# Padding the small block products of a DeltaNet inverse to 128 rows, with another load order at the start and another split of the last scaling

## The chip, the core and the metric

The kernel runs on one core of one Trainium2 chip. Its metric is the device time of one execution in microseconds (us). The engines are TensorE (PE, matrix products, with its weight loads shown apart as PEld), VectorE (DVE), ScalarE (ACT), GpSimd (POOL) and SyncE (SP), which here issues nearly all DMAs. Matrix products read SBUF and write PSUM. "L358" in the profile is the line of a helper through which nearly all instructions are recorded, so groups are told apart by the names of their tiles: `pz<-wc,dt` writes tile pz and reads wc and dt.

## What is computed

The reference is a decoder block on x of 1024 tokens by 1024 features, in float32:

```python
h = rmsnorm(x, norm1_w)
proj = h @ w_in                       # sb_q, sb_k, sb_v, sb_z, g_q, g_k, g_v, g_z, g_b, g_a
o_sb  = rmsnorm(stick_breaking_attention(sb_q, sb_k, sb_v)) * silu(sb_z)   # 8 heads of 64
o_gdn = rmsnorm(gated_delta_chunked(...)) * silu(g_z)                      # 4 heads of 128
y = x + concat(o_sb, o_gdn) @ w_out
return rmsnorm(y, final_norm_w)
```

The gated delta rule works on chunks of tokens. In each chunk a unit lower triangular system `(I + A) s = r` is solved, where A holds the decayed products of the keys with each other. The kernel uses chunks of 128 tokens, eight for each head, and forms the inverse X of the triangular matrix explicitly.

## The kernel before, in words

Large products keep float32 accuracy by splitting each operand in a high part (float32r) and a low part (the rest) and adding three products: high by high, high by low, low by high (`mm3`, lines 586 to 589). Names that end in h and l are such parts.

**The start (lines 631 to 664).** The transposed x comes in eight bands k of 128 rows (tile `xr`, 512 KB), and so does the part of the input weight that makes the attention's queries (tile `w`, named wq in the profile, 256 KB). For each band ACT makes the high parts `xh` and `wh` (wqh), DVE the low parts `xl` and `wl` (wql); x is scaled by the norm's gain on the way. Eight PSUM accumulators `qp[j]`, j = 2 i + half, hold the product for 128 columns i of the weight and one half of the 1024 tokens. Band 0 is loaded in halves, in the order: tokens 0 to 511 of x, columns 0 to 255 of the weight, tokens 512 to 1023, columns 256 to 511. Its 24 products are issued pair by pair, (0, 2), (1, 3), (4, 6), (5, 7): the second pair needs the second half of x, the third the second half of the weight. The second half's low part of x is tied behind the low part of its weight by `later` (line 654). From band 1 on each band is loaded in two DMAs and all eight accumulators take three products each.

At line 735 three DMAs clear scratch in DRAM that the inverse uses: `xd0` gets a small identity, and each `xds` gets 128 KB of zeros. They are recorded with priority 0.

**The planner.** Python simulates the engines while the program is built (classes `Model`, `Recorder`, `Pool`, lines 58 to 372, and `interleave`, line 440). Every instruction is recorded with a cost and a priority (smaller is earlier); DVE, ACT, POOL and SP each take, of the instructions that are ready in the simulation, the one with the smallest priority, and this order is written into the program for good. PE's instructions run in the order in which they are recorded. `interleave` chooses between streams (generators) whenever PE's list is empty: a stream may continue when what it waits for should have ended. Streams with priority 100 and above (the projections, and later the output's products) fill PE when no other is ready. The planner adds 150 ns where a product has another number of weight rows, in classes of 32, 64 and 128, than the one before (line 331). Once built, the order on each engine is fixed and the engines wait for each other by semaphores. A DMA of SP that comes eight DMAs later uses the same semaphore again, and waits for the older one to land.

**The inverse (`gdn_inv`, lines 1099 to 1176), once for each of four heads.** `nm` (a view of tile dt, 128x128 for each of the eight chunks) holds minus A, transposed. The inverses of the diagonal blocks of 32x32 are made by POOL and DVE and exchanged through DRAM; line 1125 loads them as `xc`, and DVE transposes each to `wc`. The blocks of 64x64 follow by products of 32x32 blocks, and from these the whole of 128x128:

- First group (lines 1137 to 1142): for both diagonal blocks of 64 rows and each of eight chunks, nm's off-diagonal block of 32x32 by wc. In the profile `pz<-wc,dt`. DVE copies the result to `y1` (tile name y).
- Second group (lines 1153 to 1160): 16 products of y1 by xc and 8 of xc by y1, which give the off-diagonal blocks and, for one of them, its transpose: `pz<-xc,y` and `pz<-y,xc`.
- Then 8 products with nm's columns 64 to 127 over all 128 rows (`pz<-wy,dt`), for which `wy` is padded with zeros, and 8 by X (`pz<-xinv,wy`).

Each of these float32 products shows as two weight loads and two matmuls, which the text calls passes.

**The end (`products_attention`, lines 1500 to 1550).** For the last block of 128 tokens the output row is cut in parts of 512, 320 and 192 columns. After each product DVE adds x, and the squares are summed (ACT for the first two, DVE for the last). POOL multiplies by the final gain (DVE for the last part), adds the sums and EPS, and takes the power -0.5 (`rsqrt`). Then line 1535 has DVE scale columns 0 to 543, line 1536 ACT columns 640 to 1023, line 1537 POOL columns 544 to 639; SP stores columns 0 to 639 and ACT's queue the rest.

Of the kernel before, what the change touches and what calls it, by code (L numbers as in the profile page):

```python
# [25 lines left out]
EPS = 1e-6  # L26
# [447 lines left out]
def block(tc, xT_d, x_d, n1_d, wE_d, wQ_d, wC_d, conv_d, alog_d, dtb_d, mixw_d, wo_d, fnw_d, out_d):  # L474
# [4 lines left out]
    with ExitStack() as top:  # L479
# [155 lines left out]
        raw, loads = [], {}  # L635
        for k in range(NK):
            w = s0.tile([P, 512], F32, tag="wcr", bufs=6, name="wq")
            wh = s0.tile([P, 512], F32R, tag="wqh", bufs=2, name="wqh")
            wl = s0.tile([P, 512], F32R, tag="wql", bufs=2, name="wql")
            xr = fx.tile([P, T], F32, f"xr{k}", "kq") if k < 4 else s0.tile([P, T], F32, name=f"xr{k}")  # L640
            raw.append(xr)
            n = 1 if k else 2
            for u in range(n):
                hs, es = slice(u * 512, T // n + u * 512), slice(u * 256, 512 // n + u * 256)
                loads.setdefault(f"k{k}", []).extend([S.dma_start(xr[:, hs], xT_d[k * P:(k + 1) * P, hs]), S.dma_start(w[:, es], wQ_d[:, k, es])])
                if k == 0 and u == 0:
                    V.tensor_copy(wh[:, es], w[:, es])
                else:
                    A.activation(wh[:, es], w[:, es], AF.Copy)
                low = V.tensor_tensor(wl[:, es], w[:, es], wh[:, es].bitcast(F32), ALU.subtract)  # L650
                A.activation(xh[:, k, hs], xr[:, hs], AF.Copy, scale=n1[:, k:k + 1])
                xlow = V.scalar_tensor_tensor(xl[:, k, hs], xr[:, hs], n1[:, k:k + 1], xh[:, k, hs].bitcast(F32), ALU.mult, ALU.subtract)
                if k == 0:
                    later(xlow, low)
            if k:
                for j in range(8):
                    i, hs = j // 2, slice((j % 2) * 512, (j % 2) * 512 + 512)
                    es = slice(i * P, (i + 1) * P)
                    mm3(qp[j], wh[:, es], wl[:, es], xh[:, k, hs], xl[:, k, hs], False, k == NK - 1)
                continue  # L660
            for pair in ((0, 2), (1, 3), (4, 6), (5, 7)):
                for a, (lw, rx) in enumerate(((wh, xh), (wl, xh), (wh, xl))):
                    for j in pair:
                        TE.matmul(qp[j], lw[:, (j // 2) * P:(j // 2) * P + P], rx[:, 0, (j % 2) * 512:(j % 2) * 512 + 512], start=a == 0, stop=False)
# [67 lines left out]
        V.memset(ones, 1.0)  # L732
        G.affine_select(triu, ones, pattern=[[1, P]], compare_op=ALU.is_ge, fill=0.0, base=0, channel_multiplier=-1)

        S.dma_start(xd0, ident[0:16, 0:16])
        V.memset(zero, 0.0)
        for t in xds:
            S.dma_start(t[0:32768].rearrange("(p u f) -> p u f", p=P, u=2), zero.unsqueeze(1).to_broadcast([P, 2, P]))
        s0_ctx.close()


# [357 lines left out]
        def gdn_inv(h):  # L1099
# [21 lines left out]
            times(yx, xa, nb)  # L1121
            times(xa[:, :, 16:32], yx, xb)
            S.dma_start(rows, xa.rearrange("p r i -> p (r i)"))
            xc = gd.tile([P, 8, 32], F32, tag="xc", name="xc")
            yield S.dma_start(xc, xd[0:32768].rearrange("(g c b r i) -> (b r) (g c) i", g=2, c=4, b=4, r=32, i=32))
            wc = gd.tile([P, 8, 32], F32, tag="wc", name="wc")
            r = V.transpose(wc.rearrange("p c i -> p (c i)"), xc.rearrange("p c i -> p (c i)"))
            wy = gd.tile([P, 8, 64], F32, tag="br", name="wy")
            W = wy[0:64]
            G.memset(W[0:32, :, 32:64], 0.0)  # L1130
            G.memset(wy[64:128], 0.0)
            V.tensor_copy(W[0:32, :, 0:32], wc[0:32])
# [2 lines left out]

            quads = [slice(32 * q, 32 * q + 32) for q in range(4)]
            y1p = pz()
            yv = y1p[:, 0:256].rearrange("p (c i) -> p c i", c=8)
            for q in range(2):
                o = 64 * q  # L1140
                for c in range(8):
                    TE.matmul(yv[o + 32:o + 64, c, :], nm(c, slice(o, o + 32), slice(o + 32, o + 64)), wc[o:o + 32, c, :], start=True, stop=True)
            y1 = gd.tile([P, 8, 32], F32, tag="yt", name="y1")
            for q in range(2):
                o = 64 * q
                r = V.tensor_copy(y1[o + 32:o + 64], yv[o + 32:o + 64])
            yield lambda: h == 0 or f"c{2 * h - 1}" in flags
            for q in range(4):
                A.activation(X[quads[q], :, quads[q]], xc[quads[q]], AF.Copy)
# [5 lines left out]
            for q in range(2):  # L1155
                o = 64 * q
                for c in range(8):
                    TE.matmul(xv[o:o + 32, c, :], y1[o + 32:o + 64, c, :], xc[o + 32:o + 64, c, :], start=True, stop=True)
            for c in range(8):
                TE.matmul(xv[32:64, c, :], xc[32:64, c, :], y1[32:64, c, :], start=True, stop=True)  # L1160
            r = V.tensor_copy(W[32:64, :, 0:32], xv[32:64])
            for q in range(2):
                o = 64 * q
# [336 lines left out]
        def products_attention():  # L1500
            yield lambda: f"d{NB - 1}" in flags
            for b in range(NB):
                last = b == NB - 1
                parts = (slice(0, 512), slice(512, 832), slice(832, D)) if last else (slice(0, 512), slice(512, D))
                sy = None
                for got in product(b, 0, parts):
                    if not isinstance(got, tuple):
                        yield got
                        continue
                    n, hs, yp, y = got  # L1510
                    if sy is None:
# [8 lines left out]
                    if last:  # L1520
                        (V if n == 2 else G).tensor_tensor(yf[:, hs], y[:, hs], wts["fnw"][:, hs], ALU.mult)
                    if n and last:
                        G.tensor_tensor(sy[:, 0:1], sy[:, 0:1], sy[:, n:n + 1], ALU.add)
                        if n == 1:
                            G.tensor_scalar(sy[:, 0:1], sy[:, 0:1], EPS, None, ALU.add)
                    elif n:
                        V.scalar_tensor_tensor(sy[:, 0:1], sy[:, 0:1], EPS, sy[:, n:n + 1], ALU.add, ALU.add)
                    if n < len(parts) - 1:
                        yield
                        continue  # L1530
                    ry = pools[0].tile([P, 1], F32, tag="ry", bufs=2, name="ry")
                    os_ = slice(b * P, (b + 1) * P)
                    if last:
                        rsqrt(ry, sy[:, 0:1], 1)
                        V.tensor_scalar(yf[:, 0:544], yf[:, 0:544], ry[:, 0:1], None, ALU.mult)
                        A.activation(yf[:, 640:D], yf[:, 640:D], AF.Copy, scale=ry[:, 0:1])
                        G.tensor_scalar(yf[:, 544:640], yf[:, 544:640], ry[:, 0:1], None, ALU.mult)
                        S.dma_start(out_d[os_, 0:640], yf[:, 0:640])
                        nc.scalar.dma_start(out_d[os_, 640:D], yf[:, 640:D])
# [57 lines left out]
```

## Time and profile before

| | us |
|---|---|
| median of 3 runs (650.01 to 651.02) | 650.99 |
| the profiled execution's own time | 651.54 |
| its span, first to last instruction | 649.6 |
| PE busy in it | 639.3 |
| DVE, ACT, POOL busy | 422.4, 393.7, 341.8 |
| PE's first product, last product's start | 1.67, 643.24 |

All rows of the profile come from that one execution, whose time is 0.55 us above the median. In a listing by time the columns are the start from the beginning of the span, the duration, the engine, the line, the operation, the tiles written and read, weights' rows*columns for PE, the shape, the number of instructions merged in the row, and in brackets the idle time ahead of it with what ended it. SPq and ACTq are the engines' issues of DMAs. PE overlaps consecutive matmuls, so what one costs is read from the distance between starts rather than from its duration.

### The profile page before, as it was taken

The page shows a single profiled execution, that of the slowest core. Times are in us where ns is not written, and L with a number is a line of the kernel's source. Part 1 is how long each engine was busy: PE and PEld are TensorE (multiplying, and loading weights), DVE is VectorE, ACT ScalarE, POOL GpSimd, SP SyncE. Part 2 cuts the span into 40 slices and gives each one's busy share as a digit, 9 for nine tenths or more (in the row PEclk, how much of TensorE's full clock was granted, in tenths as well). Part 3 has the DMA queues.
Part 4 walks back from the last instruction along what each step waited for, and adds up shares of the span by engine and source line. Part 5 has one row for each costly group of instructions (what it writes and reads, how often), then busy time and mean ns, then how long its engine had stood idle before and what let it go on. Part 6 is the DMA issues. An engine that isn't in the chain of part 4 may idle for free.

```text
span 649.6 us, 11680 instructions
## 1 busy us (share of the span) xinstructions
PE 639.3 (98%) x3976; PEld 549.7 (85%) x3976; DVE 422.4 (65%) x778; ACT 393.7 (61%) x945; POOL 341.8 (53%) x431
## 2 busy tenths in 40 slices
PE   8999999999999999999999999999999999999996
PEld 7889988988888898888888878888888888888885
DVE  4359974323877869888529887557874326568874
ACT  5745477724976869776549787467854343043553
POOL 0115046837894688835479685287731223226643
PEclk9999999999999999999999999999999999999999
DMA  8956338875383445453363752635312259953312
GB/s 302 367 207 247 115 134 272 281 222 192 95 273 128 122 140 171 141 162 102 118 212 91 267 157 85 205 107 171 112 58 82 82 195 310 346 191 107 125 75 119
DMA packets 96666, 111.82 MB, mean 172 GB/s; under 512 B 28576, under 2 KB 61536, under 8 KB 96608
## 3 DMA queue, kind: packets, MB, share of 16 engines
q1 hardware_dynamic: 96320, 110.89, 52.2%
q8 instruction: 31, 0.51, 0.3%
q14 instruction: 27, 0.22, 0.1%
q10 hardware_dynamic: 288, 0.20, 0.1%
HBM read 76.03 MB, written 35.03 MB: 171 GB/s over the span
## 4 chain that ended last, share of the span: by engine, by line
PE 91%; DVE 3%; DMA 2%; issue 1%; POOL 1%; ACT 1%; SPq 0%; POOLq 0%; DVEq 0%; ACTq 0%
PE pp L358 56%; PE pz L358 26%; PE po L358 6%; PE pc L358 3%; DVE cc L358 1%; DMA wq<-wQ 1%; DVE al L358 1%; DMA dt<-dt_s 1%; DMA kqf<-g_s 0%; SPq L358 0%; POOL sgf L358 0%; DVE wy L358 0%; POOL wel L358 0%; ACT sgf L358 0%; POOL ac L358 0%
## 5 line engine op out<-in xcount | busy, mean ns | idle before, releaser
L358 PE MATMUL pp<-xh,weh 128*128 128x512 f32 x360 | 150.2, 417 | 0.0
L358 PE MATMUL pp<-xh,wel 128*128 128x512 f32 x360 | 141.4, 393 | 0.0
L358 PE MATMUL pp<-xl,weh 128*128 128x512 f32 x360 | 141.0, 392 | 0.0
L358 POOL TENSOR_TENSOR wel<-wer,weh 128x512 fp32r<-128x512 f32 x48 | 62.6, 1312 | 87.3 <-ACT weh L358 70.9
L358 POOL TENSOR_TENSOR sgf<-sgf,cc 128x128 f32<-128x128 f32 (+3 forms) x64 | 77.4, 1212 | 49.9 <-DVE cc L358 45.2
L358 PEld LDWEIGHTS pp<-xh,wel 128*128 128x128 f32 x360 | 67.6, 188 | 15.2
L358 PEld LDWEIGHTS pp<-xl,weh 128*128 128x128 f32 x360 | 67.9, 189 | 8.6
L358 PEld LDWEIGHTS pp<-xh,weh 128*128 128x128 f32 x360 | 67.7, 188 | 8.7
L358 ACT ACTIVATE sgf<-pz,rs 128x384 f32<-128x384 f32 (+3 forms) x96 | 54.9, 606 | 7.5 <-PE pz L358 7.4
L358 DVE TENSOR_TENSOR_SCAN cc<-pz,step 128x384 f32<-128x384 f32 (+2 forms) x64 | 53.5, 847 | 8.8 <-ACT pz L358 8.0
L358 DVE TENSOR_TENSOR al<-pz,ah 128x512 fp32r<-128x512 f32 (+1 forms) x80 | 49.3, 627 | 13.3 <-ACT ah L358 12.8
L358 ACT ACTIVATE ah<-pz 128x512 fp32r<-128x512 f32 (+1 forms) x80 | 44.4, 571 | 21.0 <-PE pz L358 20.8
L358 ACT ACTIVATE pz<-pz,ns 128x384 f32<-128x384 f32 (+3 forms) x96 | 54.3, 585 | 0.0
L358 PE MATMUL pp<-woh,mh 128*128 128x512 f32 (+2 forms) x132 | 52.1, 395 | 0.0
L358 PE MATMUL pp<-woh,ml 128*128 128x512 f32 (+2 forms) x132 | 51.1, 387 | 0.0
L358 PE MATMUL pp<-wol,mh 128*128 128x512 f32 (+2 forms) x132 | 51.0, 386 | 0.0
L358 DVE SCALAR_TENSOR_TENSOR pp<-pre,conv,pp 128x512 f32<-128x512 f32 x42 | 31.4, 749 | 20.8 <-ACT pp L358 20.2
L358 POOL TENSOR_TENSOR ac<-ac,pre 128x512 f32<-128x512 f32 x24 | 31.2, 1298 | 24.1 <-ACT pre L358 14.1
L358 POOL TENSOR_TENSOR ml<-mf,mh 128x512 fp32r<-128x512 f32 x16 | 22.1, 1380 | 41.1 <-ACT mh L358 35.6
L358 PE MATMUL po<-ah,v2a 128*128 128x256 f32 (+1 forms) x160 | 41.9, 287 | 0.0
L358 DVE TENSOR_TENSOR_SCAN cc<-pz,cc,step 128x512 f32<-128x512 f32 (+1 forms) x32 | 38.8, 1211 | 2.8 <-ACT pz L358 2.4
L358 PE MATMUL po<-al,v2a 128*128 128x256 f32 (+1 forms) x160 | 38.8, 280 | 0.0
(294 smaller groups left out, 1591.3 us busy)
## 6 DMA issues: line engine op xcount, KB each, us to landing
wer<-wE SPq DMA_DIRECT2D x48, 256.0 KB, 4.1
xr<-x SPq DMA_DIRECT2D x16, 512.0 KB, 6.4
g_s<-ac SPq DMA_DIRECT2D x24, 256.0 KB, 2.2
v_s<-v2e SPq DMA_DIRECT2D x16, 256.0 KB, 2.4
kqf<-g_s SPq DMA_DIRECT2D x16, 256.0 KB, 4.9
v2a<-v_s SPq DMA_DIRECT2D x8, 512.0 KB, 5.0
q<-qk_s SPq DMA_DIRECT2D x8, 512.0 KB, 3.8
kh<-qk_s SPq DMA_DIRECT2D x8, 512.0 KB, 5.2
```

The source lines that it names most:

```text
L358: ins = f(*args, **kw).ins
```

## The change

It has three parts, and a fourth small one with the first.

1. In the inverse the operands of the two groups of small products are padded with zeros to 128 rows. `wm` and `y1` and `xm` are cleared by POOL; DVE copies two blocks of wc into `wm`, ACT two blocks of xc into `xm`. The first group becomes 8 products of a whole nm block, 128x128, by 64 columns; DVE takes the useful blocks out of the result. The second keeps its 24 products, each now over 128 rows with 32 columns of weights.
2. At the start band 0's order is: first half of x, both halves of the weight, second half of x; the pairs are (0, 2), (4, 6), (1, 3), (5, 7). For the other bands the splits are recorded weight first, and the order of their DMAs is as before. The three scratch DMAs get priority 3.
3. For the last block the last sum of squares and EPS are added on DVE in one instruction, the last part's gain is multiplied after that, and DVE scales columns 0 to 639; POOL scales none.

```diff
@@ the start
-            n = 1 if k else 2
-            for u in range(n):
-                hs, es = slice(u * 512, T // n + u * 512), slice(u * 256, 512 // n + u * 256)
-                loads.setdefault(f"k{k}", []).extend([S.dma_start(xr[:, hs], ...), S.dma_start(w[:, es], ...)])
...
+            for part, u, n in (("w", 0, 1), ("x", 0, 1)) if k else (("x", 0, 2), ("w", 0, 2), ("w", 1, 2), ("x", 1, 2)):
...
+                if k == 0 and part == "w" and u == 0:
+                    later(V.scalar_tensor_tensor(xl[:, 0, 0:512], *first_split), lows[0])
+                loads.setdefault(f"k{k}", []).append(dma)
+            if k:
+                loads[f"k{k}"].reverse()
...
-            for pair in ((0, 2), (1, 3), (4, 6), (5, 7)):
+            for pair in ((0, 2), (4, 6), (1, 3), (5, 7)):
...
+        V.memset(zero, 0.0)
+        ck.prio = 3
         S.dma_start(xd0, ident[0:16, 0:16])
-        V.memset(zero, 0.0)
         for t in xds:
             S.dma_start(t[0:32768].rearrange(...), zero.unsqueeze(1).to_broadcast([P, 2, P]))
+        ck.prio = 0
@@ gdn_inv
+            wm, xm = [gd.tile([P, 8, 64], F32, tag="tt", bufs=2, name=n) for n in ("wm", "xm")]
+            y1 = gd.tile([P, 8, 32], F32, tag="yt", name="y1")
+            for t in (wm, xm, y1):
+                G.memset(t, 0.0)
...
+            V.tensor_copy(wm[0:32, :, 0:32], wc[0:32])
+            r = V.tensor_copy(wm[64:96, :, 32:64], wc[64:96])
+            for q in range(2):
+                o = 64 * q + 32
+                A.activation(xm[o:o + 32, :, 32 * q:32 * q + 32], xc[o:o + 32], AF.Copy)
...
-                for c in range(8):
-                    TE.matmul(yv[o + 32:o + 64, c, :], nm(c, slice(o, o + 32), slice(o + 32, o + 64)), wc[o:o + 32, c, :], ...)
+            for c in range(8):
+                TE.matmul(yv[:, c, :], nm(c, slice(0, P), slice(0, P)), wm[:, c, :], start=True, stop=True)
...
-                    TE.matmul(xv[o:o + 32, c, :], y1[o + 32:o + 64, c, :], xc[o + 32:o + 64, c, :], ...)
+                    TE.matmul(xv[o:o + 32, c, :], y1[:, c, :], xm[:, c, 32 * q:32 * q + 32], start=True, stop=True)
             for c in range(8):
-                TE.matmul(xv[32:64, c, :], xc[32:64, c, :], y1[32:64, c, :], start=True, stop=True)
+                TE.matmul(xv[32:64, c, :], xm[:, c, 0:32], y1[:, c, :], start=True, stop=True)
@@ products_attention
-                    if n and last:
-                        G.tensor_tensor(sy[:, 0:1], sy[:, 0:1], sy[:, n:n + 1], ALU.add)
-                        if n == 1:
-                            G.tensor_scalar(sy[:, 0:1], sy[:, 0:1], EPS, None, ALU.add)
+                    if n == 1 and last:
+                        G.tensor_tensor(sy[:, 0:1], sy[:, 0:1], sy[:, 1:2], ALU.add)
                     elif n:
                         V.scalar_tensor_tensor(sy[:, 0:1], sy[:, 0:1], EPS, sy[:, n:n + 1], ALU.add, ALU.add)
...
-                        V.tensor_scalar(yf[:, 0:544], yf[:, 0:544], ry[:, 0:1], None, ALU.mult)
+                        V.tensor_scalar(yf[:, 0:640], yf[:, 0:640], ry[:, 0:1], None, ALU.mult)
                         A.activation(yf[:, 640:D], yf[:, 640:D], AF.Copy, scale=ry[:, 0:1])
-                        G.tensor_scalar(yf[:, 544:640], yf[:, 544:640], ry[:, 0:1], None, ALU.mult)
```

More of the change, by code (lines that the diff above doesn't have):

```diff
@@ L641, in block @@
             raw.append(xr)
-            n = 1 if k else 2
-            for u in range(n):
-                hs, es = slice(u * 512, T // n + u * 512), slice(u * 256, 512 // n + u * 256)
-                loads.setdefault(f"k{k}", []).extend([S.dma_start(xr[:, hs], xT_d[k * P:(k + 1) * P, hs]), S.dma_start(w[:, es], wQ_d[:, k, es])])
-                if k == 0 and u == 0:
-                    V.tensor_copy(wh[:, es], w[:, es])
-                else:
[L649 to L654, printed above, removed]
+            lows = []
+            for part, u, n in (("w", 0, 1), ("x", 0, 1)) if k else (("x", 0, 2), ("w", 0, 2), ("w", 1, 2), ("x", 1, 2)):
+                size = (T if part == "x" else 512) // n
+                es = slice(u * size, (u + 1) * size)
+                if part == "w":
+                    dma = S.dma_start(w[:, es], wQ_d[:, k, es])
+                    if k == 0 and u == 0:
+                        V.tensor_copy(wh[:, es], w[:, es])
+                    else:
+                        A.activation(wh[:, es], w[:, es], AF.Copy)
+                    lows.append(V.tensor_tensor(wl[:, es], w[:, es], wh[:, es].bitcast(F32), ALU.subtract))
+                else:
+                    dma = S.dma_start(xr[:, es], xT_d[k * P:(k + 1) * P, es])
+                    A.activation(xh[:, k, es], xr[:, es], AF.Copy, scale=n1[:, k:k + 1])
+                    split = [xr[:, es], n1[:, k:k + 1], xh[:, k, es].bitcast(F32), ALU.mult, ALU.subtract]
+                    if k or u:
+                        V.scalar_tensor_tensor(xl[:, k, es], *split)
+                    else:
+                        first_split = split
+                if k == 0 and part == "w" and u == 0:
[3 more added lines that the diff above has]
+                loads[f"k{k}"].reverse()
             if k:
@@ L1137, in gdn_inv @@
             y1p = pz()
-            yv = y1p[:, 0:256].rearrange("p (c i) -> p c i", c=8)
+            yv = y1p.rearrange("p (c i) -> p c i", c=8)
+            for c in range(8):
+                TE.matmul(yv[:, c, :], nm(c, slice(0, P), slice(0, P)), wm[:, c, :], start=True, stop=True)
             for q in range(2):
-                o = 64 * q
-                for c in range(8):
[L1142 to L1146, printed above, removed]
+                o = 64 * q + 32
+                r = V.tensor_copy(y1[o:o + 32], yv[o:o + 32, :, 32 * q:32 * q + 32])
             yield lambda: h == 0 or f"c{2 * h - 1}" in flags
@@ L1157, in gdn_inv @@
                 for c in range(8):
-                    TE.matmul(xv[o:o + 32, c, :], y1[o + 32:o + 64, c, :], xc[o + 32:o + 64, c, :], start=True, stop=True)
+                    TE.matmul(xv[o:o + 32, c, :], y1[:, c, :], xm[:, c, 32 * q:32 * q + 32], start=True, stop=True)
             for c in range(8):
-                TE.matmul(xv[32:64, c, :], xc[32:64, c, :], y1[32:64, c, :], start=True, stop=True)
+                TE.matmul(xv[32:64, c, :], xm[:, c, 0:32], y1[:, c, :], start=True, stop=True)
             r = V.tensor_copy(W[32:64, :, 0:32], xv[32:64])
@@ L1519, in products_attention @@
                         A.activation(junk[:, 0:hs.stop - hs.start], y[:, hs], AF.Square, scale=D ** -0.5, accum_out=sy[:, n:n + 1])
-                    if last:
-                        (V if n == 2 else G).tensor_tensor(yf[:, hs], y[:, hs], wts["fnw"][:, hs], ALU.mult)
-                    if n and last:
-                        G.tensor_tensor(sy[:, 0:1], sy[:, 0:1], sy[:, n:n + 1], ALU.add)
-                        if n == 1:
-                            G.tensor_scalar(sy[:, 0:1], sy[:, 0:1], EPS, None, ALU.add)
+                    if last and n < 2:
+                        G.tensor_tensor(yf[:, hs], y[:, hs], wts["fnw"][:, hs], ALU.mult)
+                    if n == 1 and last:
+                        G.tensor_tensor(sy[:, 0:1], sy[:, 0:1], sy[:, 1:2], ALU.add)
                     elif n:
@@ L1530, in products_attention @@
                         continue
+                    if last:
+                        V.tensor_tensor(yf[:, hs], y[:, hs], wts["fnw"][:, hs], ALU.mult)
                     ry = pools[0].tile([P, 1], F32, tag="ry", bufs=2, name="ry")
```

## The prediction

> **What bounds the kernel now.** First I read the busy times on the page and its chain of work that ended last, then what TensorE (PE) waited for, then the stretches of the span.
>
> ```profile
> span 649.6 us, 11680 instructions
> ...
> PE 639.3 (98%) x3976; PEld 549.7 (85%) x3976; DVE 422.4 (65%) x778; ACT 393.7 (61%) x945; POOL 341.8 (53%) x431
> ...
> PE 91%; DVE 3%; DMA 2%; issue 1%; POOL 1%; ACT 1%; SPq 0%; POOLq 0%; DVEq 0%; ACTq 0%
> ```
>
> ```profile
> PE po L358 <- DVE step L358: 1.7, 1, 1.7
> PE pp L358 <- DVE xl L358: 1.0, 1, 1.0
> PE pz L358 <- DVE dt L358: 0.5, 1, 0.5
> ```
>
> ```profile
> 190.00:485.00 295.00, 293.55 (x2133) 253.97 (x2133) 220.23 (x398) 212.41 (x572) 191.89 (x267) 1.00 0.47 143
> 485.00:640.00 155.00, 155.00 (x770) 128.66 (x769) 87.21 (x166) 60.63 (x127) 54.52 (x46) 1.00 0.48 164
> ```
>
> PE is busy for 98% of the span and makes 91% of the chain. Its waits are a start of 1.7 us, one stall of 1.0 us on the low half of x, and crumbs. The last view's columns are the stretch, its length, then busy time of PE, weight load, DVE, ACT and POOL: in the stretch that holds all four inverses (190 to 485) PE idles 295.00 - 293.55 = 1.45 us, and from there to 640 not at all. So I count PE time added to the inverse one for one at the end. The change can win PE time at the start and DVE/POOL time in the tail.
>
> **The start.** Eight bands of 128 rows of x and of the query weight are loaded in turn; band 0 comes in halves.
>
> ```profile
> 4.15 1.27 SPq L358 DMA_DIRECT2D xd<-smf  x2
> ...
> 5.84 0.72 ACT L358 ACTIVATE xh<-xr0f,n 128x512 fp32r<-128x512 f32 x1 [1.39 <-DMA xr0f<-xT]
> ...
> 7.01 0.39 PE L358 MATMUL pp<-xh,wqh 128*128 128x512 f32 x1
> ...
> 7.49 0.42 ACT L358 ACTIVATE wqh<-wq 128x256 fp32r<-128x256 f32 x1 [0.92 <-DMA wq<-wQ]
> ...
> 8.28 0.75 DVE L358 SCALAR_TENSOR_TENSOR xl<-xr0f,n,xh 128x512 fp32r<-128x512 f32 x1
> ...
> 9.08 0.50 PE L358 MATMUL pp<-xl,wqh 128*128 128x512 f32 x1 [0.99 <-DVE xl L358]
> ...
> 9.89 1.28 DVE L358 SCALAR_TENSOR_TENSOR xl<-xr1f,n,xh 128x1024 fp32r<-128x1024 f32 x1 [0.87 <-ACT xh L358]
> ...
> 11.10 0.68 DVE L358 TENSOR_TENSOR wql<-wq,wqh 128x512 fp32r<-128x512 f32 x1
> ...
> 12.39 0.39 PE L358 MATMUL pp<-xh,wqh 128*128 128x512 f32 x1
> ```
>
> Now x's second half is there at 5.84, but its low part waits behind the split of the second weight half, which comes at 7.49; DVE makes it at 8.28, and PE stands until 9.08. Six of band 0's 24 products are started by 7.01; band 1 begins at 12.39.
>
> After, that weight half is third in the queue and should be there by about 5.84. Six products (both x and weights ready) follow at 7.01 in place of the six that stall. Then x's second half, fourth, lands at about 7.49: its high part is done by 7.49 + 0.72 = 8.21, its low part by 8.21 + 0.75 = 8.96. At a product each 0.23 us (rows in the next part) they are due at 7.01 + 6 x 0.23 = 8.39 and 8.39 + 4 x 0.23 = 9.31, so nothing stalls, and band 1 could begin at 7.01 + 18 x 0.23 = 11.15. There the next thing is late: band 1's low weights are done at 11.10 + 0.68 = 11.78 and due two products on, at 11.61; with a hand-over of a tenth, 0.25 us. Gain 12.39 - 11.15 - 0.25 = 0.99, **1.0 us** (0.3 if x's half lands 1 us later, so that its high part stalls PE from 8.39 to about 9.3; 1.24 if nothing stalls). Three stores that prepare scratch leave SP's early queue (the two at 4.15 take 1.27 us of issue) for the place behind the small loads. The loads behind them move up; PE waits for none of them today, so I take 0. When the stores are issued later, the loads for bands 4 to 7 stand behind them; the cover is that PE had no wait there.
>
> **The inverse, per head.**
>
> ```profile
> 199.12 0.40 PE L358 MATMUL pp<-xh,wel 128*128 128x512 f32 x1
> 199.45 1.09 PE L358 MATMUL pz<-wc,dt 32*32 32x32 f32 x32
> 200.47 0.39 PE L358 MATMUL po<-ah,v2a 128*128 128x256 f32 x1
> 200.70 0.29 PE L358 MATMUL po<-al,v2a 128*128 128x256 f32 x1
> 200.82 0.28 PE L358 MATMUL po<-ah,v2a 128*128 128x256 f32 x1
> ```
>
> ```profile
> 91.59 0.40 PE L358 MATMUL pz<-xh,wel 128*128 128x512 f32 x1
> 91.82 0.53 PE L358 MATMUL pz<-smf 128*128 128x32 f32 x4
> 92.19 0.48 PE L358 MATMUL pz<-xh,weh 128*128 128x512 f32 x1
> 92.50 0.39 PE L358 MATMUL pz<-xl,weh 128*128 128x512 f32 x1
> 92.73 0.39 PE L358 MATMUL pz<-xh,wel 128*128 128x512 f32 x1
> ```
>
> ```profile
> 278.87 1.00 PE L358 MATMUL pz<-xc,y 32*32 32x32 f32 x29
> ...
> 279.80 0.57 PE L358 MATMUL pz<-y,xc 32*32 32x32 f32 x13
> ```
>
> ```profile
> 205.75 1.15 PE L358 MATMUL pz<-wy,dt 128*64 128x64 f32 x16
> ```
>
> ```profile
> L358 PE MATMUL pz<-wy,dt 128*64 128x64 f32 x64 | 4.5, 224 | 0.1
> ...
> L358 PE MATMUL pz<-y,xc 32*32 32x32 f32 x64 | 2.7, 192 | 0.0
> ```
>
> A product in float32 shows as two passes, each with its own weight load. A row's third term is the weights' rows*columns. The starts tell what a group costs, since matmuls overlap: 512 wide ones start each 0.23 us (92.73 - 92.50), 256 wide ones each 0.12.
>
> The first group, 16 products in 32 passes on 32x32 weights, stretches the step from 199.12 to 200.70 to 1.58; without it that would be 0.23 + 0.12 = 0.35. It costs **1.23 us**, of which (1.09 - 0.19)/31 = 0.029 a pass is 0.93 and the rest is getting in and out: it starts 0.33 after a 512 wide one, where 0.23 is usual, and the second matmul after it comes 0.23 later, where 0.12 is usual.
>
> After it there are 8 products, 16 passes, each with a full 128x128 block of nm as weights and 64 columns moving. No such row exists. The nearest is pz<-smf: float32, 128x128 weights, 32 columns moving. Its four passes stretch 91.59 to 92.50 to 0.91 where 0.46 is usual: 0.45, so 0.113 a pass, though 32 columns move. 16 x 0.113 = **1.81 us**. The other bound is pz<-wy,dt, 64 columns moving over weights of 64 columns: (1.15 - 0.22)/15 = 0.062 a pass, 0.99 in all. I take 0.113: a wider moving operand can't make it less, and the weights have the same shape and type. So +0.58 a head, 4 x 0.58 = **+2.3 us**.
>
> The Trainium skill ("TensorE: Matmul & The Clock Gate", LDWEIGHTS (loading the stationary operand)) says that a weight load takes columns/1.2 ns whatever the number of rows, 107 ns for 128 columns; by it 16 passes make an estimated 1.71 and the head +0.48. That speaks against this change; the 0.113 of pz<-smf agrees, and that the load rather than the moving columns sets a pass is the page's addition.
>
> The second group stays 24 products in 48 passes; its weights keep 32 columns but get 128 rows. In the row of 13 a pass takes (0.57 - 0.19)/12 = 0.032; over the group, from 278.87 to the last start at 279.80 + 0.38 = 280.18, it is 1.31/47 = 0.028, because passes of two row groups overlap where the quadrant changes (the listing alternates there). With all 128 rows in each pass I take 0.032: 47 x 0.004 = +0.19, **+0.76 us** for four heads. Bounds: 0 (overlap stays), and 0.062 a pass, +1.6 a head.
>
> Beside PE, each head gets two copies on DVE, two on ACT, three memsets on POOL.
>
> ```profile
> 197.75 0.56 DVE L358 COPY wy<-wc 32x256 f32<-32x256 f32 x2
> ...
> 198.41 1.68 ACT L358 ACTIVATE xinv<-xc 32x256 f32<-32x256 f32 x4
> ...
> 194.25 0.88 POOL L358 MEMSET wy<- 32x256 f32 x2
> ```
>
> That is 0.56 on DVE, 0.84 on ACT, about 1.3 on POOL. The memsets run while the load of xc is under way. PE's first group now waits for the DVE copies; behind it on PE's queue stands all other work, but the planner places the group only when the copies should be done and fills with projections. I cost it at 0; uncovered it is 0.56 a head.
>
> **The tail.**
>
> ```profile
> 644.32 0.35 DVE L358 TENSOR_TENSOR yf<-xr,fnw 128x192 f32<-128x192 f32 x1
> ...
> 645.42 0.50 DVE L358 TENSOR_SCALAR yf<-yf,ry 128x544 f32<-128x544 f32 x1 [0.75 <-POOL ry L358]
> 645.49 0.84 POOL L358 TENSOR_SCALAR yf<-yf,ry 128x96 f32<-128x96 f32 x1
> 646.07 0.35 ACTq L1539 DMA_DIRECT2D out<-yf  x1
> 646.36 0.33 SPq L358 DMA_DIRECT2D out<-yf  x1
> ```
>
> SP's last store waits for POOL's 96 columns (645.49 + 0.84 = 646.33). With 640 columns on DVE it waits for 645.42 + 0.50 x 640/544 = 646.01; then ACT's issue at 646.07 is the later. Gain 646.36 - 646.07 = **0.3 us**. The last small add moves from POOL to DVE, where the 0.35 multiply may stand ahead of it; it saves one engine change and risks 0.35, so 0 between -0.2 and +0.35.
>
> **Sum** against the profiled execution (span 649.6, time 651.54): -1.0 + 2.3 + 0.76 - 0.3 = +1.8 us. The median of the runs is 650.99, 0.55 below that execution; put on the median: **652.8 us**.
>
> **Rivals.**
> 1. The padding is absorbed. For it: PE idles 1.45 us between 190 and 485, and added work may fall there. Against: the idle belongs to waits that move along. +1.8 - 1.45 gives 651.3, no change. Chance 0.2.
> 2. Faster: leaving the 32-row shape is what counts, and the 128x128 loads hide behind 64 moving columns at 0.062 a pass. The first group would cost 0.99 and 0.08 for getting out (92.50 comes 0.31 after 92.19, where 0.23 is usual), 1.07, so -0.16 a head; with the second unchanged, -0.64 - 1.0 - 0.3 = -1.9, 649.0. It decides below a pass of 0.085: start and tail give 1.3, the second group takes 0.76, so the first may take (1.3 - 0.76)/4 = 0.135 a head, (1.23 + 0.135)/16 a pass. For it: the 0.1 lost on entering the 32x32 shape. Against: pz<-smf. Chance 0.13. The Trainium skill ("TensorEngine Tiling (Array Packing)", Key Properties) says that a change of tiling mode drains the array; the late entry agrees, but pz<-wy,dt still has a tiled shape, and so would the second group.
> 3. DVE's copies do hold PE up: 4 x 0.56 = 2.2 more, 655.0. For it: PE waited 0.5 on DVE ahead of one inverse already. Against: fill is ready everywhere else. Chance 0.12.
> 4. The second group runs at 0.062: 4 x 1.41 = 5.6 more, 658.4. Chance 0.05.
>
> The forecast has 0.5, with 651.9 to 654.0 as its own range. A measurement can tell 0.2%, 1.3 us, from no change. Slower by more: rivals 3 and 4 and most of the forecast, 0.60. Within: rival 1 and the forecast's lower edge, 0.25. Faster: rival 2 and a little of rival 1, 0.15. The range from 650.0 to 655.4 leaves out rival 4, the core of rival 2 and the ends of the others. The planner also writes a new order for all engines, which may move some tenths either way.
>
> **What would show it.** Start: the 1.0 wait on xl gone, band 1 at about 11.4. First group: rows of 128*128 with 128x64, 16 passes in about 1.8 us; passes under 0.085 would refute me. Second: 48 passes in some 1.5. Tail: no yf scaling on POOL, both stores issued near 646.07 less the shift of the end. Stretch 190 to 485: PE idle still about 1.5; far more would be rival 3, near none rival 1.

## The result and the profile after

The changed kernel takes 655.83 us (median of 5 runs, 655.67 to 656.27), the kernel before 650.99 (5 runs, 650.01 to 651.57): a ratio of 1.0073, with an interval of 1.0062 to 1.0084, so 4.8 us slower. The forecast was 652.8, with a range from 650.0 to 655.4. The profiled execution after took 656.27, its span is 654.5. First the page's busy times and chain.

```profile
span 654.5 us, 11590 instructions
...
PE 642.7 (98%) x3912; PEld 552.2 (84%) x3912; DVE 431.8 (66%) x787; ACT 399.3 (61%) x953; POOL 344.1 (53%) x440
...
PE 91%; DVE 4%; POOL 2%; issue 1%; DMA 1%; ACT 1%; SPq 0%; POOLq 0%; DVEq 0%; ACTq 0%
```

PE still sets the end: its busy time grew by 3.4 us (639.3 before) with 64 passes fewer, and the span by 4.9. Next, what PE waited for (total, times, longest), and the two stretches that the prediction used.

```profile
PE po L358 <- DVE step L358: 1.7, 1, 1.7
PE pz L358 <- DVE dt L358: 1.0, 1, 1.0
PE pz L358 <- DVE oe L358: 0.9, 2, 0.4
PE pp L358 <- DVE xr L358: 0.8, 1, 0.8
```

```profile
190.00:485.00 295.00, 292.56 (x1982) 252.99 (x1982) 224.93 (x399) 216.23 (x576) 195.83 (x277) 1.00 0.48 144
485.00:640.00 155.00, 154.22 (x838) 128.61 (x836) 88.12 (x170) 59.67 (x125) 53.53 (x45) 1.00 0.48 161
```

The wait of 1.0 on xl is gone, as it should be. In its place PE idles 295.00 - 292.56 = 2.44 us in the stretch of the inverses, where it was 1.45, and 0.78 later, where it was nothing. The granted clock is 1.00 in both.

**The start**, in order of time:

```profile
6.98 0.72 ACT L358 ACTIVATE xh<-xr0f,n 128x512 fp32r<-128x512 f32 x1 [0.72 <-DMA xr0f<-xT]
...
11.14 0.49 PE L358 MATMUL pp<-xh,wqh 128*128 128x512 f32 x1 [0.35 <-ACT wqh L358]
...
11.31 0.69 DVE L358 TENSOR_TENSOR wql<-wq,wqh 128x512 fp32r<-128x512 f32 x1
...
12.05 0.51 PE L358 MATMUL pp<-xh,wql 128*128 128x512 f32 x1
...
12.40 0.39 PE L358 MATMUL pp<-xh,wqh 128*128 128x512 f32 x1
```

The pairs run in the order that was forecast, x's second half lands at 6.98 (forecast 7.49) and band 1 begins at 11.14 (11.15). That these two agree is luck. In this trace the first products stand 0.23 us apart from 5.05 on, where they stood 0.43 apart until 6.53 before, so band 0's last product starts at 10.40 already and band 1 was due at 10.63. But band 1's weight is late, 0.35 for the high part ahead of 11.14, and then the low part, so that the third product starts at 12.05 where 11.14 + 0.46 = 11.60 was due. The fourth, at 12.40, stood at 13.07 before: the gain in this trace is 0.7.

**The inverse of the first head**: PE's rows, then those of DVE and POOL just ahead of them.

```profile
198.96 0.39 PE L358 MATMUL pp<-xh,wel 128*128 128x512 f32 x1
200.31 1.97 PE L358 MATMUL pz<-wm,dt 128*128 128x64 f32 x16 [0.96 <-DVE dt L358]
202.09 0.48 PE L358 MATMUL pp<-xh,weh 128*128 128x512 f32 x1
202.40 0.39 PE L358 MATMUL pp<-xl,weh 128*128 128x512 f32 x1
...
204.56 0.98 PE L358 MATMUL pz<-xm,y 128*32 128x32 f32 x29 [0.44 <-DVE oe L358]
...
205.47 0.58 PE L358 MATMUL pz<-y,xm 128*32 128x32 f32 x13
```

```profile
196.62 0.87 POOL L358 TENSOR_TENSOR sgf<-sgf,cc 128x384 f32<-128x384 f32 x1
196.68 2.26 DVE L358 COPY wm<-wc 32x256 f32<-32x256 f32 x2
197.44 1.35 POOL L358 TENSOR_TENSOR kqf<-kqf,cb 128x512 f32<-128x512 f32 x1
198.96 0.58 DVE L358 COPY wy<-wc 32x256 f32<-32x256 f32 x2
199.55 0.61 DVE L358 SCALAR_TENSOR_TENSOR dt<-pz,mr2b,dt 128x128 f32<-128x128 f32 x2
```

One pass of the first group costs (1.97 - 0.27)/15 = 0.113 us, the last matmul's own 0.27 taken off: the forecast to the third place. With the idle of 0.96 taken out, the step from 198.96 to 202.40 is 2.48; two steps of 0.23 less, the group costs 2.02 where 1.81 was forecast and 1.23 was before. Taken so at all four heads, the groups cost about 7.8 us together where they cost 4.9 before. The second group lasts from 204.56 to its last start at 205.47 + 0.38 = 205.85, so 1.29 us: no more than the 1.31 of before, though each pass has all 128 rows. The forecast had put the short passes of before down to an overlap of two row groups; here they are as short without a change of row group. And the two wm copies, priced at 0.56 us, take 2.26 beside two instructions of POOL; dt, the products' weights, stands behind them in DVE's queue, and PE waits 0.96 for it, and 0.44 more ahead of the second group.

**The tail**, in order of time:

```profile
647.84 0.28 PE L358 MATMUL pp<-woh,ml 128*128 128x192 f32 x1
...
649.43 0.54 POOL L358 TENSOR_TENSOR ry<-sy,half 128x1 f32<-128x1 f32 x1 [0.98 <-DVE sy L358]
650.01 0.62 ACT L358 ACTIVATE yf<-yf,ry 128x384 f32<-128x384 f32 x1 [1.99 <-POOL ry L358]
650.01 0.55 DVE L358 TENSOR_SCALAR yf<-yf,ry 128x640 f32<-128x640 f32 x1 [0.66 <-POOL ry L358]
650.59 0.33 SPq L358 DMA_DIRECT2D out<-yf  x1
650.65 0.35 ACTq L1557 DMA_DIRECT2D out<-yf  x1
```

The later store is issued 650.65 - 647.84 = 2.81 us after the last product's start; before it was 646.36 - 643.24 = 3.12. That is the 0.3 of the forecast, but the span ends 3.85 after that issue, where it ended 3.24 after it.

### The profile page after: what moved, and what is told of

It is laid out like the page before. It is cut to its first block, busy times and chain, and to the rows that moved or that the text cites. A ratio compares the mean times of both kernels' runs of the same rounds, so it can differ in the third digit from the quotient of the medians.

```text
span 654.5 us, 11590 instructions
## 1 busy us (share of the span) xinstructions
PE 642.7 (98%) x3912; PEld 552.2 (84%) x3912; DVE 431.8 (66%) x787; ACT 399.3 (61%) x953; POOL 344.1 (53%) x440
## 4 chain that ended last, share of the span: by engine, by line
PE 91%; DVE 4%; POOL 2%; issue 1%; DMA 1%; ACT 1%; SPq 0%; POOLq 0%; DVEq 0%; ACTq 0%
PE pp L358 55%; PE pz L358 26%; PE po L358 7%; PE pc L358 3%; DVE cc L358 1%; DMA xr1f<-xT 1%; POOL sgf L358 1%; DVE wm L358 0%; DVE wy L358 0%; POOL ac L358 0%; POOL wel L358 0%; DVE xr L358 0%; DVE pp L358 0%; DVE al L358 0%; SPq L358 0%
```

## The experiments

Each ratio is to the kernel before on the same chip. Theory A: the forecast's terms are right in kind, and the padding costs its passes and its waits. Its rivals came up on the way: that the copies hold PE up (C), that the price is the load of 128 weight columns (L), and that any new order of the same instructions moves the time (O).

**One part at a time.** e1 has the inverse's part of the diff alone, e2 the start's, e3 the tail's, e4 both of the latter.

> Only the padding of the inverse, with start and tail as before. Theory A (the padding costs PE time: the first group's passes wait for 128-column weight loads, some 0.75 us a head by the rows of the changed kernel, and the longer solve makes PE idle): 5.0 to 5.8 us over before, as start and tail were worth about 0.7 together. Theory B (the new order that the planner writes for the whole kernel costs the time, whichever edit causes it): the three parts done alone each cost something, and this one clearly less than 4.8.

> Only the new load order at the start. Theory A: 0.7 us less than before, as band 1 begins 1.25 us earlier (11.14 for 12.39) and 0.5 of it is given back to the wait for band 1's low weights; 650.3. Theory B: the planner's new order costs some us after 90, so 652 or more.

> Only the other split of the last scaling. Theory A: between 0.4 us less and no change (the last store of SP is issued 0.37 us earlier after the last product, ACT's only 0.02). Theory B: no change too, as the plan ahead of the tail stays.

> Start and tail of the change without the padding. Theory A: 0.7 to 1.1 us less than before, about 650.0, the best version of these. Theory B: as in the run with the start alone, 652 or more.

| | us | ratio and interval |
|---|---|---|
| e1, padding alone | 656.75 | 1.0083 (1.0069 to 1.0096) |
| e2, start alone | 650.23 | 0.9985 (0.9976 to 0.9994) |
| e3, tail alone | 651.20 | 1.0000 (0.9991 to 1.0009) |
| e4, start and tail | 650.34 | 0.9989 (0.9980 to 0.9998) |

The start gives 1.0 us (0.4 to 1.6), as forecast. In e2's trace nothing stalls there: band 1 begins at 10.93 and its fourth product at 11.61, 1.46 earlier than before, so the gain differs from one execution to the next. The tail's 0.3 can't be told from nothing. The padding alone costs 5.5 us where 3.1 was forecast. e2 has the lowest time, faster than both kernels, and e4 can't be told from it. In the traces of e2, e3 and e4 PE's products stand in before's order but for band 0 itself; e1's leave that order from about 182 us on, ahead of the first head's inverse. So only the padding brings a new order of PE with it, and these four runs can't tell its passes from that order.

**The load of 128 columns.** e5 is the changed kernel with the first group as 16 products with 32 weight columns.

```diff
-                TE.matmul(yv[:, c, :], nm(c, slice(0, P), slice(0, P)), wm[:, c, :], ...)
+                for c in range(8):
+                    TE.matmul(yv[o:o + 32, c, :], nm(c, slice(0, P), slice(o, o + 32)), wm[:, c, 32 * q:32 * q + 32], ...)
```

> The changed kernel, with the first group's products padded to 128 rows too but cut to 32 columns of weights and 32 moving columns: 16 products instead of 8. Theory L (a pass waits for its 128-column weight load): a pass falls from 0.115 us to about 0.03, the group from 1.8 to about 1.05, so 4 x 0.75 = 3.0 us less than the changed kernel, 652.8. Rival (128 rows, or the row class, make the pass slow): the group takes 1.7 or more, no gain, 655.8.

657.48 us, 1.0089 (1.0076 to 1.0102): no gain. Yet its groups are short again: 32 passes start within 0.88 to 0.90 us, 0.029 a pass. But the planner wrote another order for it, and PE waits longer than in the changed kernel. So L could not be judged by the time of a kernel that is planned anew. f1 and f5 repair this: the kernel before with the first group in either form, where the planner is told the old cost, so that before's order stays (in f1 a few rows around the last head's inverse are exchanged; in f5 none). Both leave out the zero padding, so their numbers are not the reference's.

```diff
-                    TE.matmul(yv[o + 32:o + 64, c, :], nm(c, slice(o, o + 32), slice(o + 32, o + 64)), wc[o:o + 32, c, :], ...)
+f1          for c in range(8):
+f1              u = min(c, 6)
+f1              TE.matmul(yv[:, c, :], nm(c, slice(0, P), slice(0, P)), wc[:, u:u + 2, :].rearrange("p c i -> p (c i)"), ...)
+f5                  TE.matmul(yv[o + 32:o + 64, c, :], nm(c, slice(0, P), slice(o + 32, o + 64)), wc[:, c, :], ...)
```

> The kernel before, in its own order of all engines, with the first group of each head's inverse alone in the changed form: 8 products of 128 rows by 128 weight columns with 64 columns moving, where before had 32 of 32 rows. It leaves out the zero padding (whole rows of the old tiles stand in for the padded ones), so its numbers are not the reference's; the time is that of the passes. No added copy, no memset, no new order. Theory P (a first group costs 0.75 us more a head, the 7.10 against 4.07 us of four heads in the two profiles, and what e1 lost beyond that is the re-written order): 2.4 to 3.2 us over before. Theory W (nearly all of e1's 5.5 us is the groups themselves, through what waits behind them): 4.5 us or more over before.

> As the run above in all else, with the first group as 16 products of 128 rows by 32 weight columns with 32 columns moving, in before's own order of all engines; it leaves out the zero padding too. Theory L (the pass costs what its load of 128 weight columns costs; with 32 weight columns it is 0.03 us): the groups last as before, within 0.7 us of before, so that the 7.2 us over before in e5 were its order and not its products. Rival (128 rows are dear whatever the columns): as f1, 2.4 us or more over before.

The group's row of the three kernels, by shape: before, f1, f5.

```profile
L358 PE MATMUL pz<-wc,dt 32*32 32x32 f32 x128 | 4.3, 192 | 0.5 <-DVE dt L358 0.5
```

```profile
L361 PE MATMUL pz<-wc,dt 128*128 128x64 f32 x64 | 7.7, 274 | 0.5 <-DVE dt L361 0.5
```

```profile
L361 PE MATMUL pz<-wc,dt 128*32 128x32 f32 x128 | 4.4, 197 | 0.5 <-DVE dt L361 0.5
```

f1 takes 652.87, 1.0031 (1.0019 to 1.0042): 2.0 us over before (1.2 to 2.7). Theory P had expected 2.4 to 3.2. f5 takes 651.49, 1.0003 (0.9994 to 1.0012): no difference, with all 128 rows in each pass. So L holds: 128 weight rows cost nothing here, and 128 weight columns cost the 2.0 us. f1 also moves 64 columns where f5 moves 32, but that isn't the price: pz<-smf took 0.113 a pass with 32 columns moving over 128 weight columns, and pz<-wy,dt 0.062 with 64 moving over 64. P's other half follows in kind: about 3 of e1's 5.5 us are not passes (3.5 by f1's time, 2.6 by the steps of e1's own groups, which cost 7.8 where they cost 4.9).

**The copies.** e6 is the kernel before with the memsets and the four copies added and the products as they were; e9 is the changed kernel with wm's copies on ACT; f3 is the whole padding in before's order, with the planner told that the copies cost nothing.

```diff
+e6        (gdn_inv's added memsets, V.tensor_copy and A.activation of the change; its products not)
-e9        V.tensor_copy(wm[0:32, :, 0:32], wc[0:32])
+e9        A.activation(wm[0:32, :, 0:32], wc[0:32], AF.Copy)
+f3        self.fake, self.zero: costs of before for the group, none for the copies
```

> The kernel before with only the helpers of the padding: the three memsets, the two copies on DVE ahead of the first group, the two on ACT; products as before, the padded tiles are read by nobody. Theory C (what the padding costs beyond its 3.0 us of passes is PE waiting for these copies, which POOL's work on the shared access to SBUF stretches): 1.2 to 2.4 us over before, 652.5 to 653.7. Rival (the copies are covered and the rest is the planner's order): within 0.7 of before.

> The changed kernel with the two copies that fill wm made by ACT instead of DVE. Theory C: the waits of 0.96 and 0.41 ahead of the first group go, 1.0 to 1.8 us less than the changed kernel, 654.0 to 654.8. Rival (the planner's order): no less than 655.3.

> The whole padding of the inverse, with its memsets and copies, as in e1, but the planner is told before's costs for the group and none for the copies, so that nearly all of before's order stays (rows around the last head's inverse are exchanged). Theory P: f1's loss plus what PE waits for the copies where they are on its way; 3 to 5 us over before. If the copies are covered, as the prediction had it: equal to f1 within 0.6 us. If it is the padding itself and not the order that costs e1's 5.5 us: 5 to 6 us over before.

All three are worse than the changed kernel: e6 660.69, 1.0141 (1.0114 to 1.0169); e9 659.94, 1.0121 (1.0107 to 1.0135); f3 661.70, 1.0166 (1.0149 to 1.0182). For e6 and f3 this is above everything that was expected of them. e6 and e9 are new orders with new waits (1.3 of dt at the third head in e6; 2.4 on zt, far from the inverse, in e9), so their times can't price the copies. But e6 shows what the copies do at the first head. It has the narrow products of before, and PE waits there as in the changed kernel, behind the same pair of copies:

```profile
197.12 2.26 DVE L358 COPY wm<-wc 32x256 f32<-32x256 f32 x2
...
200.74 1.07 PE L358 MATMUL pz<-wc,dt 32*32 32x32 f32 x32 [0.92 <-DVE dt L358]
```

f3 keeps before's order up to the exchanged rows: its waits, its rows at the second head, and stretches with PE's granted clock as third number from the end.

```profile
PE pz L361 <- DVE wm L361: 2.5, 2, 1.9
PE po L361 <- DVE step L361: 1.7, 1, 1.7
PE pz L361 <- POOL sgf L361: 1.4, 2, 1.0
```

```profile
275.39 1.18 DVE L361 TENSOR_TENSOR_SCAN cc<-pz,step 128x512 f32<-128x512 f32 x1
...
276.50 1.48 DVE L361 COPY wm<-wc 32x256 f32<-32x256 f32 x2
276.69 1.14 POOL L361 TENSOR_TENSOR sgf<-sgf,cc 128x512 f32<-128x512 f32 x1
...
278.13 2.44 PE L361 MATMUL pz<-wm,dt 128*128 128x64 f32 x16 [1.87 <-DVE wm L361]
280.32 0.56 PE L361 MATMUL po<-ah,v2a 128*128 128x256 f32 x1
```

```profile
276.00:278.00 2.00, 0.26 (x4) 0.12 (x2) 1.97 (x3) 1.94 (x6) 2.00 (x3) 1.00 0.20 77
...
280.00:281.00 1.00, 1.00 (x6) 1.00 (x6) 0.40 (x1) 0.00 (x0) 0.00 (x0) 0.50 0.59 209
```

In before's order a scan of 1.18 us stands between the transpose and the copies, the copies are stretched to 1.48, and PE waits 1.87 for them. Then its clock is granted at half for some 3.4 us (279.5 to 282.9), and the po products start 0.21 to 0.36 apart instead of 0.12. The 1.4 on sgf stand ahead of the first head's inverse, where POOL has the new memsets between its instructions. f3 takes 8.8 us more than f1, and the clock is the smaller part of it, as f3's execution with a mean clock of 0.999 took 660.52. So in that order the copies and memsets together cost several microseconds, not 0: the cover that the prediction named has to be made by the planner, which pays for it by another order. What that costs is the next question.

**Another order of the same work.** e7 sets the planner's charge for a change of weight rows to 0; p1, q3 and q4 set its slack (how long a result should have been ready before a stream goes on) to 460, 440 and 470 ns. Nothing is added or left out.

```diff
-                at += 150
+e7              at += 0
-SLACK = 450
+p1 SLACK = 460      (q3: 440, q4: 470)
```

> The kernel before with one number of the planner changed: no 150 ns for another class of rows. The work stays, only the order that the planner writes changes. Theory: an order as good as any other costs under 1 us, 650.3 to 652.3. Rival (any new order costs this kernel us, since the old one was picked): 652.5 or more.

> The kernel before with one constant of the planner changed (its slack of 450 ns made 460), so that it writes another order of the same work; no instruction is added or left out. Theory O (any other order of this work loses some us, as e7's lost 2.5, because before's is one that was picked): 1 to 4 us over before. Rival (e7's order was worse for a reason of its own): within 0.7 us of before.

> The changed kernel with the planner's slack of 450 ns made 460: the same instructions in another order, to stand beside p1, the kernel before with the same constant (1.0090). Theory O (the change is worth its passes, some 1.5 us, less the start's 1.0, and the rest of its 4.8 us is which order the planner came to): 655 to 660 us, so near p1's time, within 3 us to either side. Theory D (the change itself costs 5 us, copies and waits with it, whatever the order): 5 us over p1, 661 us or more.

> The changed kernel with the slack at 440 ns, to stand beside the next run. Theory O: within 3 us of it, either way. Theory D: 4 to 6 us over it.

> The kernel before with the slack at 440 ns: a third order of the same work. Theory O (the order that before has is a good one of many): 653 to 658 us, as e7 and p1. If e7 and p1 were chance: within 0.7 us of before.

> The changed kernel with the slack at 470 ns, a fourth order of it. Theory O: anywhere from 653 to 661 us. Theory D: from 656 us up, 5 us over what before gives with the same constant.

> The kernel before with the slack at 470 ns, the partner of the changed kernel's 658.0 us (1.0104). The pairs so far give after less before 4.8 us (450), 2.1 (460) and 2.4 (440). Theory O: 652 to 658 us, so a difference of 0 to 6. Theory D (5 us in each pair): 653 us.

Medians in us, with the ratio to the unaltered kernel before. With e7's constant the changed kernel's order comes out the same as without it, so its first time stands in both rows.

| planner's constant | before | changed | difference |
|---|---|---|---|
| as it was (slack 450) | 650.99 | 655.83, 1.0073 (1.0062 to 1.0084) | 4.8 |
| no charge for rows (e7) | 653.99, 1.0032 (1.0020 to 1.0044) | 655.83 | 1.8 |
| slack 440 | 652.35, 1.0029 (1.0013 to 1.0045) | 654.76, 1.0054 (1.0041 to 1.0067) | 2.4 |
| slack 460 | 656.36, 1.0090 (1.0068 to 1.0112) | 658.49, 1.0112 (1.0099 to 1.0125) | 2.1 |
| slack 470 | 657.56, 1.0096 (1.0081 to 1.0110) | 658.01, 1.0104 (1.0091 to 1.0117) | 0.5 |

The differences are those of the medians, each good to one or two microseconds, and in the rows e7, 460 and 470 the two kernels ran on different chips. Ten or twenty nanoseconds in one constant cost the kernel before 1.9 to 6.3 us (0.0029 to 0.0096 of 651), and p1's loss is above the 1 to 4 us that theory O gave it. The change costs 0.5 to 4.8, 2.3 in the mean of the five rows; with this spread that mean is good to about 2 us (an estimate from the five differences). Theory D, a cost of 5 us in each pair, falls. At slack 440 the loss of the kernel before is mostly the clock's: its execution with a mean clock of 0.999 took 650.83, no more than the unaltered kernel. At slack 460 it isn't: the fastest, at 0.997, took 655.28. What the order does is to be seen in PE's waits, here of p1 and of the kernel before at slack 470:

```profile
PE pz L358 <- DVE al L358: 1.7, 2, 1.3
PE po L358 <- DVE step L358: 1.7, 1, 1.7
PE pp L358 <- ACT weh L358: 1.3, 1, 1.3
```

```profile
PE pp L358 <- DVE zt L358: 2.3, 1, 2.3
PE pz L358 <- DVE al L358: 1.7, 2, 1.3
```

These waits lie at other places than the inverse's products, and the unaltered kernel has none of their size but the 1.7 and 1.0 of the start.

**The planner's price of a wide product.** It books a pass of the first group at half of what it takes. e8 is the changed kernel with the load in its cost.

```diff
-        return 2 * max(n / 1.2, 20) + 3
+        return 2 * max(n / 1.2, 20, 0.86 * size(args[1])) + 3
```

> The changed kernel with the planner's cost of a product raised to 0.86 ns a weight column and pass where that is more than its moving columns cost, so that it knows the price of the load of 128 columns. Rival (the planner, which books a pass of the first group at 0.055 us, packs too tightly behind it, and that is the loss beyond the passes): 652 to 654 us. Theory O (a better cost only makes another order): anywhere from 653 to 661 us.

656.34 us, 1.0081 (1.0067 to 1.0094): the rival falls. PE's wait at the first groups goes down to 0.2 us, but it waits for ml, mh and xr elsewhere. At the first head POOL runs one instruction beside wm's copies instead of two; they take 1.25 us, and PE doesn't wait:

```profile
196.11 0.87 POOL L358 TENSOR_TENSOR sgf<-sgf,cc 128x384 f32<-128x384 f32 x1
196.17 1.25 DVE L358 COPY wm<-wc 32x256 f32<-32x256 f32 x2
...
198.78 1.97 PE L358 MATMUL pz<-wm,dt 128*128 128x64 f32 x16
```

## Why the prediction was wrong

- **Start, -1.0:** right by e2, whose interval (0.4 to 1.6) also holds the 0.7 of the trace after; there band 1's low weight costs 0.45 where 0.25 was allowed, and its high part is late as well.
- **First group, +2.3:** the mechanism was right, a load of 128 columns in each pass (f5 against f1), and 0.113 a pass was exact. In before's order it is worth 2.0 (f1).
- **Second group, +0.76:** 0; passes with 128 rows are as short as those with 32 were.
- **Tail, -0.3:** the store is issued 0.3 earlier, and the time doesn't show it; the interval of e3, 0.6 to either side, holds both.
- **Copies at 0:** wrong. Rival 3 had the right place, but its price, the bare 0.56 of the copies at each head, isn't what showed: the copies are stretched beside POOL, at the first head above all. In five orders that hold the whole change or the padding alone (the changed kernel, e1, slack 440, 460, 470) PE waits 0.9 to 1.4 us ahead of the first groups, 0.92 to 0.97 of it at the first head; in the five orders of before it waits 0, 0, 0, 0.5 and 1.3, and never at the first head. e6, with the copies and before's products, waits there too (0.92), and e8 and f3, where POOL runs less or nothing beside the copies of the first head, don't. So the copies beside POOL's work are the cause of that wait. e9 waited there with wm's copies on ACT too, because wy's copies took their place beside POOL:

```profile
196.54 2.25 DVE L358 COPY wy<-wc 32x256 f32<-32x256 f32 x2
197.31 1.34 POOL L358 TENSOR_TENSOR kqf<-kqf,cb 128x512 f32<-128x512 f32 x1
```

- **The step that failed** is that PE's waits were put at almost nothing, in two places: the copies "at 0", which cost about 1 us, and the sentence "The planner also writes a new order for all engines, which may move some tenths either way." With no change in the work another order cost the kernel before 1.9 to 6.3 us, and in all four tries it cost, never gained. Rebuilt from the runs the change is worth -1.0 + 2.0 + about 1 = +2, near the 2.3 of the five pairs. That the forecast's sum of +1.8 is near it too is partly luck, as the 0.76 of the second group, which was nothing, stands where the copies' 1 us is missing. The other 2.5 us or so of the 4.8 are put down to the order by difference, not measured: before's is the best of its five samples, and the padding trades it for another.

The rows of the two traces can also be added up without the pairs. The first groups cost 2.9 us more in the changed kernel's own order, PE idles 1.0 more in the stretch of the inverses and 0.8 more behind it (on xr, at 557), the start gives 0.7, and from the last product's start to the end of the span it takes 0.3 more: 4.3 of the span's 4.9. PE's clock has no share in this, as it is 1.00 from the stretch of the inverses up to the last products in both.

What stays open: how the orders' times are spread beyond five samples each, and how much of any one order's loss is which wait. A padded kernel in an order as good as before's was not found.

## What to carry to other kernels

Where a static planner writes the order, a change at one place can re-draw all that follows (the padding did, start and tail did not): time an unchanged kernel under two or three meaningless changes of a planner's constant first, take that spread as the range, and compare variants in pairs or with the order held. Padding a product's rows was free on PE here and padding its weight columns was not, so pad the contraction and keep the columns narrow. Copies that feed a product are hidden only if a queue has room ahead of it, so look at what stands behind them on their own engine.

## What the runs showed of the hardware

- **The granted clock can fall to half behind a PE wait of a few microseconds or less.** At slack 440 the kernel before shows this, first PE's row and then stretches with its granted clock as third number from the end:

```profile
389.83 1.09 PE L358 MATMUL pz<-wc,dt 32*32 32x32 f32 x32 [1.32 <-DVE al L358]
```

```profile
390.00:392.00 2.00, 2.00 (x42) 1.96 (x40) 1.96 (x4) 0.00 (x0) 0.75 (x1) 1.00 0.00 0
392.00:399.00 7.00, 7.00 (x74) 5.54 (x74) 4.31 (x8) 3.79 (x15) 2.79 (x3) 0.52 0.39 122
```

The stretches at half clock last about 3.4 us (f3) or 6.8 (here), and in the same kernel they come in some executions and not in others: twelve of it took 650.83 us at a mean clock of 0.999 up to 656.70 at 0.989. In the 20 traces seven of them stand ahead of the program's end, each beginning within 2.4 us of the end of such a wait (3.0, 2.4, 2.3, 1.9, 1.3, 1.3 us, and in e6 two of 0.7); waits of 1.3 or 1.4 in e6, e7 and p1 have none behind them. That the wait is the cause is argued from this, and no run tried it by itself. The Trainium skill ("TensorE: Matmul & The Clock Gate", What's actually happening) says that the clock is halved after an idle window of about 3.4 us; the lengths agree, but here the clock fell after 1.3 us of idle.
- **A pair of DVE copies from SBUF to SBUF beside POOL's work ends about 0.15 us after POOL's instruction does.** In the changed kernel the pair of wm copies ends at 196.68 + 2.26 = 198.94 and POOL's second instruction at 197.44 + 1.35 = 198.79; in f3 the ends are 277.98 and 277.83, in e9 (wy's copies) 198.79 and 198.65. With POOL idle the wy pair of the changed kernel takes 0.58. In e8 POOL's one instruction ends at 196.11 + 0.87 = 196.98 and the pair at 197.42, so that one of the two copies, half of 0.58, came after it. The Trainium skill ("SBUF — State Buffer", Who interferes with whom) states a port pair that the two lock for a whole instruction; the rows agree, and no run tried it by itself.
